# MLP products in a Strassen form on 2x2 blocks, tokens in two passes

## The chip, the cores and the metric

The kernel runs on one core of one Trainium2 chip, as one program. The metric is the device time of one execution in microseconds. The engines are TensorE (PE; its weight loads are shown as PEld), VectorE (DVE), ScalarE (ACT), GpSimd (POOL) and SyncE (SP), which issues nearly all DMAs from one queue, in order.

## The reference, cut to what matters

One layer of a decoder trunk for 2048 tokens of width 1024, all in float32. The change touches the W_out product, the MLP and the gated embeddings; what stands ahead of them (8 heads of softmax attention with a forget gate, "FoX", and 4 heads of a chunkwise "mLSTM") stays the same in what it computes.

```python
def reference(x, p, w_in, ..., w_up, w_down, w_ple, g_ple, w_ple_gate, g_final):
    ...
    mix = jnp.concatenate([fox_out, ml_out], axis=-1).astype(x.dtype)
    x = x + mix @ w_out[i]                                        # 2048x1024 @ 1024x1024

    hm = rmsnorm(x, g_mlp[i])
    x = x + jnp.square(jax.nn.relu(hm @ w_up[i])) @ w_down[i]     # 1024 -> 4096 -> 1024

    gate = jax.nn.sigmoid(rmsnorm(x, g_ple[i]) @ w_ple_gate[i])   # 1024x1024
    x = x + gate * (p[i] @ w_ple[i])
    return rmsnorm(x, g_final)
```

## The kernel before, in words

A float32 product is made of three float16 matmuls: each factor is split into a high half (the value rounded to float16) and a low half (the rest), and `PASSES` takes high x high, high x low, low x high. So one product of a 128-deep slice costs three matmuls, and every factor has to be split first: ACT writes the high half, DVE or POOL subtracts it for the low one.

The stages follow one another: norm of x and its transposes; four mLSTM heads (`ml_z` projects a head, `gates` makes the gate sums, then a loop over 16 chunks of 128 tokens); attention in pairs of heads, with a share of W_out between; the rest of W_out (`o`, L642 by `wo_token`); the MLP; the gates (`pg`, L991); the final norm.

The MLP goes over 16 blocks `jb` of 256 hidden columns. For each, `mlp_w` loads 1 MB of w_up (`prep_w`) and 1 MB of w_down (`prep_rows`) and makes a power-of-two scale, high and low halves, all of it while the block before is at work. `mlp_up` makes the hidden block of a group of 512 tokens (48 matmuls of 128x512, L1011), squares its relu and splits it; `mlp_down` multiplies it by the rows of w_down (48 matmuls, L1029) and adds each 128x512 result to x in SBUF (L1034). All 2048 tokens of x stay in SBUF (`x1`). The gates stage loads and splits w_ple_gate in four column blocks of 256 and runs 16 tokens tiles on each.

A scheduler sets the order of the instructions on each engine when the program is built, from the order in the source and from what it expects each to take; the buffers of a pool (`bufs=`) decide which load may start when. At run time every engine goes through its own list in order and waits at semaphores. The staging tile `st` has one buffer that all weight loads share.

## Time and profile before

| | us |
|---|---|
| median of 3 runs (lowest to highest) | 2996.92 (2991.71 to 3000.48) |
| profiled execution, span from first to last instruction | 2998.0 |
| norm, transposes | 0 to 33.6 |
| mLSTM, first part of it the projections of head 0 | 33.6 to 530 |
| attention and the first half of W_out | 530 to 1347 |
| second half of W_out, MLP | 1347 to 2784 |
| gates and final norm | 2784 to 2998 |

The profile lists each instruction with its engine, its line of the kernel and its tile. A chain of waits goes back from the last instruction to what released each one; a timeline merges like instructions into a row with its start, its duration and a count (x48). Busy times of PE overlap within a row, since matmuls are pipelined: what 48 of them cost is read from the start of one row to the start of the next.

### The profile page before, as it was taken

Reading aid. Unit: us, or ns where it says so; the run is one execution under the profiler, and the core shown is the slowest. Engines: PE = TensorE matmul, PEld = TensorE weight load, DVE = VectorE, ACT = ScalarE, POOL = GpSimd, SP = SyncE. Lnnn points to the kernel's source line nnn. Section 1 sums busy time; section 2 is a strip of 40 time slices with the busy share of each in tenths; the row PEclk is TensorE's granted clock in tenths of the full one; section 3 lists DMA queues with packets and bytes.
Section 4 is the critical chain, followed back from the end, with each engine's and each line's share of the span. In section 5 each row is a group of like instructions: output and inputs, shape, how many; then the busy total and the mean of one; then the engine's idle time right before and its main releaser. Section 6 shows DMA issues by size and latency. Waiting matters only on the chain. (4 is left out here: it accounts for less than half of the span.)

```text
span 2998.0 us, 43441 instructions
## 1 busy us (share of the span) xinstructions
PE 2747.0 (92%) x17141; PEld 1483.3 (49%) x17141; DVE 1676.0 (56%) x3764; ACT 1049.3 (35%) x1878; POOL 751.9 (25%) x529
## 2 busy tenths in 40 slices
PE   4998999889888787888899999999999999999996
PEld 2766767454453443443344444444444444444785
DVE  6464654666858667557754454444544544445526
ACT  6244444465655564553411111111111111114432
POOL 1001100233433343243122111111121111111454
PEclk9999999999999998999999999999999999999998
DMA  9112220486876797896700000000000000003513
GB/s 246 38 44 57 57 50 22 112 156 131 146 148 132 150 200 187 190 201 218 149 29 29 29 29 29 15 26 17 29 29 28 29 29 29 28 15 70 112 43 141
DMA packets 539869, 256.27 MB, mean 85 GB/s; under 512 B 433296, under 2 KB 511376, under 8 KB 539664
## 3 DMA queue, kind: packets, MB, share of 16 engines
q1 hardware_dynamic: 529904, 236.67, 34.8%
q10 hardware_dynamic: 9760, 16.82, 1.7%
q8 instruction: 134, 2.20, 0.3%
q14 instruction: 71, 0.58, 0.1%
HBM read 113.88 MB, written 32.60 MB: 49 GB/s over the span
## 5 line engine op out<-in xcount | busy, mean ns | idle before, releaser
L1029 PE MATMUL d<-wd_hl,hid 128*128 128x512 f16 x3072 | 677.2, 380 | 10.7 <-DVE x L1034 10.6
L1011 PE MATMUL h<-y1t,wu_hl 128*128 128x512 f16 x3072 | 673.5, 379 | 2.5 <-ACT y1y L201 2.5
L1029 PEld LDWEIGHTS <-hid 128*128 128x128 f16 x3072 | 301.1, 98 | 376.6 <-issue 16.8
L1011 PEld LDWEIGHTS <-wu_hl 128*128 128x128 f16 x3072 | 300.5, 98 | 365.2 <-ACT y1y L201 3.0
L1034 DVE SCALAR_TENSOR_TENSOR x<-d,fac,x 128x512 f32<-128x512 f32 x512 | 373.5, 747 | 132.2 <-PE d L1029 132.1
L1019 POOL TENSOR_TENSOR hid<-r,hid 128x512 f16<-128x512 f32 x128 | 174.7, 1365 | 772.3 <-ACT hid L1018 666.4
L1017 DVE SCALAR_TENSOR_TENSOR r<-h,r 128x512 f32<-128x512 f32 x128 | 88.3, 690 | 461.6 <-ACT r L1015 461.5
L1015 ACT ACTIVATE r<-h 128x512 f32<-128x512 f32 x128 | 76.0, 594 | 768.9 <-PE h L1011 768.9
L812 POOL TENSOR_TENSOR ph<-sp,ph 128x1024 f16<-128x1024 f32 x119 | 255.8, 2162 | 311.5 <-ACT ph L810 216.3
L272 PEld LDWEIGHTS <-yt 128*128 128x128 f16 x3072 | 245.0, 100 | 37.0 <-issue 15.0
L261 PE MATMUL zqk<-yt,wqk_hl 128*128 128x512 f16 x768 | 188.0, 392 | 27.0 <-DMA yt<-yy 27.0
L805 ACT ACTIVATE sp<-sp,nb,fs 128x1024 f32<-128x1024 f32 (+3 forms) x192 | 179.1, 982 | 50.4 <-DVE nb L802 34.9
L991 PE MATMUL pg<-wpg_hl,y2t 128*128 128x256 f16 x1536 | 173.3, 276 | 17.6 <-ACT emb L1110 13.6
L272 PE MATMUL zvo<-wvo_hl,yt 128*128 128x256 f16 x1536 | 174.7, 275 | 4.8 <-ACT wvo_hl L156 3.5
L782 PE MATMUL s<-K,Q 128*128 128x512 f16 (+3 forms) x320 | 117.5, 367 | 62.7 <-DVE mx L790 61.1
L991 PEld LDWEIGHTS <-y2t 128*128 128x128 f16 x1536 | 151.9, 99 | 39.1 <-issue 19.7
L810 ACT CAST ph<-sp 128x1024 f16<-128x1024 f32 x136 | 139.0, 1038 | 71.5 <-DMA pt<-ph 71.3
L827 PE MATMUL av<-vt,pt 128*128 128x129 f16 x1088 | 115.5, 229 | 49.2 <-DVE og L837 29.3
L790 DVE CUSTOM_DVE_ANT_0 sp<-s,bias,mx 128x512 f32<-128x512 f32 (+2 forms) x192 | 124.0, 646 | 17.8 <-POOL ph L812 5.1
L827 PEld LDWEIGHTS <-pt 128*128 128x128 f16 x1088 | 102.8, 102 | 53.1 <-issue 31.9
L261 PEld LDWEIGHTS <-wqk_hl 128*128 128x128 f16 x768 | 77.4, 101 | 104.0 <-ACT wqk_hl L156 24.9
L642 PEld LDWEIGHTS <-mix 128*128 128x128 f16 x768 | 74.1, 101 | 99.9 <-issue 26.8
(378 smaller groups left out, 3581.3 us busy)
## 6 DMA issues: line engine op xcount, KB each, us to landing
x<-in_x_dram SPq DMA_DIRECT2D x32, 512.0 KB, 4.6
wu_st<-in_w_up_dram SPq DMA_DIRECT2D x16, 1024.0 KB
wd_st<-in_w_down_dram SPq DMA_DIRECT2D x16, 1024.0 KB, 4.9
bias<-crow SPq DMA_DIRECT2D x16, 512.0 KB, 5.1
pled<-fox_st ACTq DMA_DIRECT2D x32, 256.0 KB, 3.0
wod<-spare ACTq DMA_DIRECT2D x32, 256.0 KB, 3.5
wos<-wod SPq DMA_DIRECT2D x32, 256.0 KB, 3.5
emb<-pled SPq DMA_DIRECT2D x64, 128.0 KB, 2.1
```

Of the source, the lines that this page charges most:

```text
L261: PE.matmul(ps, lhsT=hl[:, a, kt, m * P:(m + 1) * P], rhs=yT[g][b][:, kt, :], start=i == 0, stop=i == 3 * KT - 1)
L272: PE.matmul(ps[:, 0:n], lhsT=yT[g][b][:, kt, o:o + P], rhs=hl[:, a, kt, 0:n], start=i == 0, stop=i == 3 * KT - 1)
L790: V.tensor_tensor_reduce(out=st[u][:, o * P:(o + n) * P], in0=ps[:, 0:n * P], in1=bias[kb // 8][:, kb % 8 * P:(kb % 8 + n) * P], scale=1.0 ...
L805: A.activation(sl_, sl_, AF.Exp, bias=nb, scale=fs[:, 0:1])
L810: A.copy(ph[:, 0:1024], st[u])
L812: eng.tensor_sub(ph[:, 1024:2048], st[u], ph[:, 0:1024])
L827: PE.matmul(ar, lhsT=pt[:, o, :], rhs=vs, start=kb == 0, stop=False)
L991: PE.matmul(ps, lhsT=aT[t // 4][ya][:, kt, o:o + P], rhs=hl[:, wa, kt, :], start=i == 0, stop=i == 3 * KT - 1)
L1011: PE.matmul(ps, lhsT=wu[:, a, kt, m * P:(m + 1) * P], rhs=y1T[g][b][:, kt, :], start=i == 0, stop=i == 3 * KT - 1)
L1019: T.tensor_sub(hid[:, 1, m], r2, hid[:, 0, m])
L1029: PE.matmul(ps, lhsT=hid[:, a, m, t * P:(t + 1) * P], rhs=wd[:, b, m, hf * 512:(hf + 1) * 512], start=i == 0, stop=i == 5)
L1034: V.scalar_tensor_tensor(xs, ps, fac, xs, ALU.mult, ALU.add)
```

## The change

Both MLP products are made from 2x2 blocks. Of a product of blocks, eight block products become seven, on sums and differences of the blocks (`ORD_U`, `ORD_D`: the order in which the seven are made). The token side of a block pair is a pair of groups of 512 tokens, so the MLP runs in two passes over two groups each (`PAIRS`), and x of one pass at a time stays in SBUF; the other lies in DRAM (`xd`).

The sums of the weights are made once, in the first pass, for 16 blocks of w_up (`up_prep`) and 16 of w_down (`down_prep`): load 1 MB into the one buffer `raw`, scale it in place, make four sums, split seven blocks into halves of one buffer `poa` (`po()` gives its two halves in turn), and write them to DRAM (`wud`, `wdd`). Both passes read them back, 256 KB per step of w_up (`u_load`, three buffers) and 512 KB per two steps of w_down (`d_load`, two buffers). Since all sums need one common scale, `w_max` first reads all of both matrices for their largest value, in the chunk loops of the mLSTM, two 1 MB loads per four chunks.

W_out is done pass by pass, both column halves of a token tile together. The seven token blocks of the first pass are transposed into SBUF (`y_prep_sb`), those of the second are made from x in DRAM by way of `raw` and `poa`, written to DRAM (`y_prep_dr`) and loaded when the second pass starts. A step of the MLP is 12 matmuls of 128x512; steps of up and down alternate, those of down 17 steps behind. There are 32 x 7 steps of up and 2 x 8 x 7 x 2 of down. The gates run per token tile with all 1024 columns, on weights that are loaded and split during the last steps of down (`pg_prep`).

```diff
+    def w_max(i):
+        n, dn = divmod(i, 2)
+        st = wst.tile([P, 2 * D], F32, tag="st", name=f"mxs{i}", bufs=1)
...
+            V.tensor_reduce(mxd[:, n:n + 1], st, axis=AX.X, op=ALU.max,
+                            apply_absolute_value=True)
...
                 A.activation(jk, num[:, c, 0:MD], AF.Square, accum_out=ss[:, c:c + 1])
+                if c % 2 == 1:
+                    w_max(8 * h + c // 2)
...
+    raw = sl.tile([P, 2 * D], F32, tag="u", name="raw", bufs=2)
+    poa = sl.tile([P, 4 * D], F16, tag="u", name="poa", bufs=2)
...
+    def split(dst, src, every=0):
+        A.copy(dst[0], src)
+        cnt_lo[0] += 1
+        eng = V if every and cnt_lo[0] % every == 0 else T
+        eng.tensor_sub(dst[1], src, dst[0])
...
+    def up_prep(n):
...
+        SP.dma_start(out=raw.rearrange("p (k f) -> p k f", k=KT),
+                     in_=w_up[:, n * 256:(n + 1) * 256].rearrange("(k p) n -> p k n", p=P))
+        yield
+        for k in range(KT):
+            A.activation(raw[:, k * 256:(k + 1) * 256], raw[:, k * 256:(k + 1) * 256], AF.Copy,
+                         scale=msc[:, k:k + 1])
...
+        V.tensor_add(s4(sd, 0), a(1, 0), a(1, 1))
+        V.tensor_sub(s4(sb, 0), s4(sd, 0), a(0, 0))
+        yield
+        V.tensor_sub(s4(sb, 1), a(0, 0), a(1, 0))
+        V.tensor_sub(s4(sd, 1), a(0, 1), s4(sb, 0))
+        out_(pt, 0, 2)
+        yield
+        pt2 = po()
+        split(pair_hl(pt2), sb, 2)
+        yield
+        out_(pt2, 2, 2)
+        pt = po()
+        split(pair_hl(pt), sd, 2)
+        yield
+        out_(pt, 4, 2)
+        pt2 = po()
+        v = pt2[:, 0:D].rearrange("p (a k f) -> p a k f", a=2, k=4)
+        A.copy(v[:, 0], a(1, 1))
+        T.tensor_sub(v[:, 1], a(1, 1), v[:, 0])
+        yield
+        out_(pt2, 6, 1)
...
+    def y_prep_dr(t, rs):
...
+        def dst(k, t_, pt):
+            n = len(k)
+            st = po().rearrange("p (i s) -> p i s", s=P)[:, 0:8 * n]
+            SP.dma_start_transpose(out=st, in_=pt[:, 0:n * D])
+            SP.dma_start(out=ycd[k][:, :, t_ * P:(t_ + 1) * P], in_=st)
...
+    def u_step(k):
...
+        for kt in range(4):
+            for a, b in PASSES:
+                PE.matmul(ps, lhsT=wt[:, a, kt, :], rhs=yt[:, b, kt, :],
+                          start=fresh and m == 0, stop=m == 11,
+                          skip_group_check=True)
+                m += 1
+        u_load(k + 3)
...
+    for k in range(NU + OFF):
+        if k < NU:
+            n, pos = divmod(k, 7)
+            u_step(k)
+            if n == NF - 1:
...
+                SP.dma_start(out=Y[pk][:, 8 * j:8 * j + 8], in_=ycd[pk][:, 8 * j:8 * j + 8])
...
+        if k >= OFF:
+            d_step(k - OFF)
+        if k < NF * 7 - 7:
+            credit += BG_RATE
+            while credit >= 1:
+                credit -= 1
+                next(bg, None)
...
-    for b in range(4):
-        cs = slice(b * 256, (b + 1) * 256)
-        hl, pw = prep_w(w_ple_gate, [(b * 256, 256)], g_ple_t, f"wpg{b}")
```

On SP after the transposes of the first norm, before (`wqk`, `wvo`: weights of the next mLSTM head; `crow`, `mrow`, `wt`: gate rows on their way to DRAM and back):

```order
L128 DMA wqk_st<-in_w_in_dram 128x8x128 x2
L128 DMA wvo_st<-in_w_in_dram 128x8x128 x2
L380 DMA crow<-scr_1070 128x128
L128 DMA wqk_st<-in_w_in_dram 128x8x128 x2
L411 DMA mrow<-scr_1070 64x128
L491 DMA wt_1551<-mrow 128x16x128
```

and now, at the same place (`mxs`: the loads of `w_max`):

```order
L439 DMA mxs_1588<-in_w_up_dram 128x8x256
L433 DMA mxs_1631<-in_w_down_dram 128x2x1024
L439 DMA mxs_1674<-in_w_up_dram 128x8x256
L433 DMA mxs_1717<-in_w_down_dram 128x2x1024
L439 DMA mxs_1760<-in_w_up_dram 128x8x256
L433 DMA mxs_1803<-in_w_down_dram 128x2x1024
L439 DMA mxs_1846<-in_w_up_dram 128x8x256
L433 DMA mxs_1889<-in_w_down_dram 128x2x1024
L128 DMA wqk_st<-in_w_in_dram 128x8x128 x2
L380 DMA crow<-scr_1073 128x128
L128 DMA wvo_st<-in_w_in_dram 128x8x128 x2
L411 DMA mrow<-scr_1073 64x128
```

Eight loads of 1 MB that share the one staging buffer now stand ahead of the weights of head 1. On PE at this place 151 matmuls of the projections of head 1 (`zqk`) stood between the end of `gz` and the first chunk product of head 0 (`n`, L505 before), and now there are 95.

On SP in the middle of the first pass, one block of w_down on its way (`wring_16410` is the ring of `u_load`, `wring_16411` that of `d_load`, `wud_` and `wdd_` the sums in DRAM); before, one load of w_up and one of w_down stood here per block:

```order
L1133 DMA raw<-in_w_down_dram 128x2x1024
L1339 DMA wring_16411<-wdd_15674 128x2048
L1328 DMA wring_16410<-wud_15662 128x1024 x2
L1143 DMA wdd_15675<-poa 128x2x1024
L1339 DMA wring_16411<-wdd_15674 128x2048
L1143 DMA wdd_15675<-poa 128x2x1024
L1328 DMA wring_16410<-wud_15663 128x1024
L1143 DMA wdd_15675<-poa 128x2x1024
L1143 DMA wdd_15675<-poa 128x1024
L1133 DMA raw<-in_w_down_dram 128x2x1024
```

Loads into `raw`, writes of sums and loads for PE are now interleaved in one queue. From the first step of up on, 29 loads into `raw` for blocks of weights stand there, one to some 3.5 loads of `u_load`.

On SP where the second pass starts (`y_`: token blocks in SBUF, `ycd_`: the same in DRAM, `wud_15657`: block 0 of w_up again); before, nothing of the kind was there:

```order
L1239 DMA_TRANSPOSE poa<-poa 128x16x128
L1573 DMA y_16008<-ycd_15682 128x4096
L1240 DMA ycd_15683<-poa 2048x1x128
L1573 DMA y_16008<-ycd_15682 128x4096
L1239 DMA_TRANSPOSE poa<-poa 128x8x128
L1573 DMA y_16009<-ycd_15683 128x4096
L1240 DMA ycd_15684<-poa 1024x1x128
L1573 DMA y_16009<-ycd_15683 128x4096
L1573 DMA y_16010<-ycd_15684 128x4096
L1328 DMA wring_16410<-wud_15657 128x1024 x3
```

The last token blocks are transposed, written and loaded back ahead of the loads for the second pass. On PE all steps of down of the first pass stand ahead of the first step of up of the second.

## Rows read from the trace of the kernel before

**Rows 1.** The page: span, and what DMA moved in 40 equal slices.
```profile
span 2998.0 us, 43441 instructions
GB/s 246 38 44 57 57 50 22 112 156 131 146 148 132 150 200 187 190 201 218 149 29 29 29 29 29 15 26 17 29 29 28 29 29 29 28 15 70 112 43 141
```

**Rows 2.** Busy time by stage: stretch, length, PE, PEld, DVE, ACT, POOL, PEclk, DMA, GB/s.
```profile
1500.00:2784.00 1284.00, 1282.31 (x5936) 580.62 (x5935) 617.60 (x951) 230.70 (x341) 234.94 (x169) 1.00 0.10 29
2784.00:2998.00 214.00, 173.47 (x1538) 151.85 (x1536) 96.79 (x218) 70.70 (x209) 108.58 (x131) 0.93 0.36 101
```

**Rows 3.** The chain of waits in the MLP: start, duration, what.
```profile
2606.24 10.36 PE h L1011 x48
```

**Rows 4.** The chain of waits, where it leaves PE for one block.
```profile
2199.60 5.49 DMA wu_st<-in_w_up_dram
```

**Rows 5.** Groups by line and shape: count, busy time, mean ns, idle time before.
```profile
L812 POOL TENSOR_TENSOR ph<-sp,ph 128x1024 f16<-128x1024 f32 x119 | 255.8, 2162 | 311.5 <-ACT ph L810 216.3 <-DVE mx L790 26.1 <-DVE nb L802 25.3
...
L1019 POOL TENSOR_TENSOR hid<-r,hid 128x512 f16<-128x512 f32 x128 | 174.7, 1365 | 772.3 <-ACT hid L1018 666.4 <-issue 105.9
...
L810 ACT CAST ph<-sp 128x1024 f16<-128x1024 f32 x136 | 139.0, 1038 | 71.5 <-DMA pt<-ph 71.3
...
L1017 DVE SCALAR_TENSOR_TENSOR r<-h,r 128x512 f32<-128x512 f32 x128 | 88.3, 690 | 461.6 <-ACT r L1015 461.5
...
L1018 ACT CAST hid<-r 128x512 f16<-128x512 f32 x128 | 79.1, 618 | 118.3 <-DVE r L1017 118.3
...
L165 DVE TENSOR_REDUCE wd_mx<-wd_st 128x1 f32<-128x2048 f32 x16 | 36.5, 2283 | 1.4 <-DMA wd_st<-in_w_down_dram 1.2
...
L168 ACT ACTIVATE wd_hl<-wd_st,wd_sc 128x2048 f16<-128x2048 f32 x16 | 32.0, 2002 | 169.1 <-DVE wd_sc L121 157.8 <-DVE fac L1046 11.1 <-DMA y1t<-y1y 0.2
...
L1110 ACT ACTIVATE emb<-pg,invg 128x256 f32<-128x256 f32 x64 | 29.0, 457 | 4.3 <-PE pg L991 4.3
```

**Rows 6.** DMA issues: tiles, queue, count, size, median us from issue to landing.
```profile
wd_st<-in_w_down_dram SPq DMA_DIRECT2D x16, 1024.0 KB, 4.9
...
mixd<-mT SPq DMA_DIRECT2D x8, 512.0 KB, 3.4
...
y1t<-y1y SPq DMA_TRANSPOSE x16, 4.8
```

**Rows 7.** Timeline of PE around the gate sums: start, duration, what, [idle before].
```profile
136.72 12.49 PE L261 MATMUL zqk<-yt,wqk_hl 128*128 128x512 f16 x46
149.05 0.49 PE L357 MATMUL cps<-scr 128*128 128x192 f32 x2
...
163.09 12.47 PE L261 MATMUL zqk<-yt,wqk_hl 128*128 128x512 f16 x57
179.84 0.80 PE L505 MATMUL n<-va,wt 128*128 128x129 f32 x2 [4.28 <-DVE wt L502]
```

**Rows 8.** Timeline of SP's queue, same place.
```profile
80.00 1.00 SPq L128 DMA_DIRECT2D wqk_st<-in_w_in_dram  x2
```

**Rows 9.** Timeline of PE in W_out and at the MLP's start.
```profile
1347.01 41.83 PE L642 MATMUL o<-wo_hl,mix 128*128 128x512 f16 x192
...
1408.12 22.52 PE L642 MATMUL o<-wo_hl,mix 128*128 128x512 f16 x96 [5.55 <-DVE x L1069]
1433.13 10.52 PE L1011 MATMUL h<-y1t,wu_hl 128*128 128x512 f16 x48 [2.49 <-ACT y1y L201]
```

**Rows 10.** Timeline of SP's queue in the transposes of y.
```profile
1421.06 31.64 SPq L204 DMA_TRANSPOSE y1t<-y1y  x12
```

**Rows 11.** Timeline of PE: end of the MLP, and the last gate matmuls.
```profile
2784.14 5.40 PE L991 MATMUL pg<-wpg_hl,y2t 128*128 128x256 f16 x48
...
2972.32 2.78 PE L991 MATMUL pg<-wpg_hl,y2t 128*128 128x256 f16 x24 [1.47 <-ACT emb L1110]
```

**Rows 12.** Timeline of POOL, same columns, in W_out.
```profile
1372.08 3.59 POOL L150 TENSOR_TENSOR wu_st<-wu_st,wu_gs 128x2048 f32<-128x2048 f32 x1 [8.62 <-issue]
```

**Rows 13.** Timeline of DVE at the same moment.
```profile
1372.48 3.74 DVE L1075 TENSOR_TENSOR x<-x,wos 128x512 f32<-128x512 f32 x1 [3.80 <-DMA wos<-wod]
```

More of the change, by code (lines that the diff above doesn't have):

```diff
@@ new lines, in chain, with take @@
+    def chain(*gens):
+        for g_ in gens:
+            yield from g_
+    def take(gen, n):
+        for _ in range(n):
+            if next(gen, 0) == 0:
+                return False
+        return True
+    gen = chain(up_prep(0), up_prep(1))
+    for h in range(2):
+        for t in range(4):
+            wo_tok(0, h, t)
+            take(gen, 2)
+    y_tiles()
+    r0_ = rstds(ssx[0], "y1")
+    rs0 = [r0_[:, 0:4], r0_[:, 4:8]]
+    gen2 = chain(*(y_prep_sb(t, rs0) for t in range(4)))
@@ new lines, in hybrid_layer @@
+    take(gen, 99)
+    for h in range(2):
+        for t in range(4):
+            wo_tok(1, h, t)
+            take(gen2, 4)
+    take(gen2, 99)
+    r1_ = small.tile([P, 8], F32, tag="rs1", name="rs1", bufs=1)
+    V.tensor_copy(r1_, rstds(ssx[1], "y1b"))
+    rs1 = [r1_[:, 0:4], r1_[:, 4:8]]
+    hA = [tp.tile([P, 16, GT], F16, tag="T", name=f"hid{i}") for i in range(2)]
+    hB = wst.tile([P, 4 * D], F16, tag="st", name="hid2", bufs=1)
+    wA = whl.tile([P, 4 * D], F16, tag="hl", name="wring0", bufs=2)
@@ new lines, in hybrid_layer, with x_pair, gate_tok @@
+    xg = [whl.tile([P, 2, D], F32, tag="hl", name=f"xg{i}", bufs=2) for i in range(2)]
+    xg.append(wst.tile([P, 2, D], F32, tag="st", name="xg2", bufs=1))
+    nxg = [0]
+    def x_pair(h, q):
+        v = xg[nxg[0] % 3]
+        nxg[0] += 1
+        rows = slice((4 * h + 2 * q) * P, (4 * h + 2 * q + 2) * P)
+        SP.dma_start(out=v, in_=xd[0][rows, :].rearrange("(j p) c -> p j c", p=P))
+        return v
+    def gate_tok(pi, h, t, xt):
+        g = PAIRS[pi][h]
+        tok = 4 * g + t
+        yt = y2T[pi, h]
+        emb = qt(f"emb{tok}").rearrange("p i c -> p (i c)")
+        gate = qt(f"gate{tok}").rearrange("p i c -> p (i c)")
+        SP.dma_start(out=emb, in_=pled[tok * P:(tok + 1) * P, :])
+        ps = mmp.tile([P, 2, GT], F32, tag="d", name=f"pg{tok}", bufs=2)
+        for c in range(2):
+            m = 0
@@ new lines, in gate_tok @@
+                    m += 1
+            for i in range(2):
+                cs = slice(c * GT + i * 256, c * GT + (i + 1) * 256)
+                A.activation(gate[:, cs], ps[:, c, i * 256:(i + 1) * 256], AF.Sigmoid,
+                             scale=pwg_[2 * c + i])
+            cs = slice(c * GT, (c + 1) * GT)
+            T.tensor_mul(gate[:, cs], gate[:, cs], emb[:, cs])
+        V.tensor_add(xt, xt, gate)
+        A.activation(emb, xt, AF.Square, accum_out=ss3[:, tok:tok + 1])
+        T.tensor_mul(xt, xt, gfin)
@@ new lines, in hybrid_layer @@
+    pend = None
+    seq = [(pi, h, q) for pi in range(2) for h in range(2) for q in range(2)]
+    side = None
+    xq = {s: x_pair(s[1], s[2]) for s in seq[:3]}
+    for n, (pi, h, q) in enumerate(seq):
+        if pi:
+            xt = X[h][q]
+        else:
+            xt = xq.pop((pi, h, q))
+        if n == 0:
+            side = y2_sb(0)
+        if n == 2:
+            y2b[1] = yp.tile([P, 16, GT], F16, tag="y45", name="y2_1")
+            side = chain(side, y2_sb(1))
+        for j in range(2):
+            gate_tok(pi, h, 2 * q + j, xt[:, j])
+            next(side, None)
+            if n < 2:
+                pass
+        gate_end(pi, h, 2 * q + 1, xt)
+        if n + 3 < 4:
+            xq[seq[n + 3]] = x_pair(*seq[n + 3][1:])
+        if n == 3:
+            take(side, 99)
```

600 lines of the change are left out of this document (474 added, 126 removed).

## The prediction, made before the changed kernel ran

> **What bounds the kernel now.** I read the busy times by stage first, then the chain of waits, then PE's timeline at both edges of the MLP. From 1500 to 2784 us PE is busy 1282.3 of 1284 us at full granted clock; DVE, ACT and POOL have half or less [rows 2]. The chain agrees: it runs on PE alone, 10.36 us for 48 matmuls, 0.2158 us each [rows 3]. So this stage goes down in proportion to matmuls, as long as everything else stays under PE. At the edges it is otherwise: between the first W_out matmul at 1347.0 and the first gate matmul at 2784.1 lie 1437.1 us, and 6528 matmuls (384 of W_out, 6144 of the MLP) take 1408.8, so some 28 us are waits, the longest 5.55 and one of 2.49 for the first y [rows 9]. The gates stage takes 214 us, of which PE is busy 173 [rows 2]; 23 us follow the last gate matmul, which ends at 2975.1 [rows 11].
>
> **The change, part by part**, against the profiled span of 2998.0 us, 1.1 above the median of the runs shown.
>
> *Matmuls of the MLP.* 224 steps of up and 224 of down with 12 matmuls are 5376 for 6144: -768 x 0.2158 = **-165.7 us**. That is the whole gain, if PE never waits.
>
> *The maxima of the weights.* 32 loads of 1 MB, each with a DVE reduction, through one staging buffer: load 4.9 [rows 6] plus reduction 2.28 [rows 5], some 7.7 us each with the hand-over. Eight stand on SP ahead of the weights of head 1, whose load was issued at 80.0 [rows 8]; it now goes out at about 80 + 8 x 7.7 = 142, and its split weights are there some 18 us later (load 4.9, reduction 2.3, scaling by POOL 3.6 [rows 12], cast and subtraction 2 each, and small ones). At 136.7 PE used to go straight into the projections of head 1, 151 matmuls up to the first chunk product at 179.8 [rows 7]. Now it waits from 136.7 to about 149 for the gate sums, and to about 160 for the weights; of the 151 only 95 stand there, so 56 x 0.2158 = 12 us are done later, and the product itself comes a few us late: 14 to 18. Later, three chunk loops have 14 chunks in all without projections as filler, at six fillers or 1.3 us each: 17. Sum **+32**; from +10 (the chunk loops absorb it) to +60 (each of the four loops waits for its last loads).
>
> *W_out and the start.* The same 384 matmuls, 82.9 us. The seven blocks of the first pass are made under the second half of them, 41 us: 12 full transposes and 4 half ones, at 31.64/12 = 2.64 us [rows 10] 37 us; but each full one waits for one of two halves of `poa`, held for a cast 1.04, a subtraction 2.16 and a transpose 4.8, so 4 us apiece at best, 58 in all [rows 5, 6]. PE then waits 15 to 25 us. Before, this place had the 28 us of waits. I set the two equal: **0**, from -15 to +15.
>
> *First pass: the preparation of the weights.* It is a chain through one buffer `raw`, and on SP its loads stand in between those that PE needs, so PE can't run away from it: with three buffers of 256 KB it is at most three steps ahead. For w_up: load 5.49 [rows 4]; eight scalings of 128x256 at 0.457; three dependent sums at 0.69; cast 1.04; low half 2.16; then the write of that half of `poa`, 512 KB, 3.4; then the last block, cast 0.62 and low half 1.37, the last readers of `raw` [rows 5, 6]. Sum 19.7. For w_down the scaling is one instruction of 2.0 and the load 4.9: 17.6. Mean **18.7 us**. PE itself needs 24 x 0.2158 = 5.18 us for a step of up and one of down, and 3.5 such steps per load into `raw`: 18.1. So chain and PE are nearly level in the first pass.
>
> 29 blocks remain after the first step of up; then four tokens' blocks of the second pass, each three full rounds and a short one of transpose 4.8 and write 3.4 through the two halves of `poa` (28.6) and load, scaling and first split (7): 36; then a reload of 1 MB, 4.9. All that stands ahead of the second pass: 29 x 18.7 + 4 x 36 + 5 = 691 us. PE's own work there is 224 x 12 x 0.2158 = 580. So **+111 us**, mostly a gap at the end of the first pass, where only the tokens' blocks are left. Bounds: 18.1 per block, as PE paces it, and 29 per token give 646 (+66); 22.5 per block gives 802 (+222).
>
> *Second pass.* No preparation; DMA goes at 1.84 MB for up and as much for down per 36 us, 101 GB/s, where the start of this kernel moved 246 [rows 1]. DVE has per 36 us some 13 operations of 128x512 at 0.69 and 7 of twice that width, 19 us in all [rows 5]. **0**.
>
> *Gates.* 768 matmuls of 128x512, 165.7 us, where 1536 of 128x256 stand in 191 us from 2784.1 to 2975.1 [rows 11]; the weights are made under the last steps of down. Tail: sigmoid, product, sum and final scale of a whole row, which I estimate at 16 for 23. With 4 for the start: 186 for 214, **-28**; between -35 and -10.
>
> Sum: -165.7 + 32 + 0 + 111 - 28 = -51: span 2947, a run of **2946 us**.
>
> A rule that speaks against this. On the trace: a POOL multiplication of 3.59 us began at 1372.08, and a DVE addition of two SBUF tiles that began at 1372.48 ended with it after 3.74 us [rows 12, 13], though such an operation takes 0.69 [rows 5]. The Trainium skill, "SBUF — State Buffer" (Who interferes with whom), states it as a rule: DVE's second SBUF input and POOL go through one port pair, an exclusive lock. The trace agrees; what it would give is the second rival.
>
> **The rivals.**
>
> *Preparation hidden* (faster still). If low halves fall to DVE where POOL is busy, and casts never wait on ACT, the chain is PE's 18.1 and a token's blocks 29: +66. With +10 for the maxima and -10 for the start: -165.7 + 66 + 10 - 10 - 28 = -128, **2870 us**. For it: all durations used are means that hold waits. Against it: the order itself puts all steps of down of the first pass ahead of the second, which says that the tokens' blocks are late in any case.
>
> *The first pass turns into a queue of small waits* (slower). Per pair of blocks, 36 us of PE, POOL has some six subtractions of 128x1024 and five of 128x512, 20 us [rows 5]; DVE has 15 operations of 128x512 and two or three wider ones on two SBUF tiles, 14 us. If one blocks the other, as in rows 12 and 13, each of the five such operations on a block's chain can wait for a foreign one of up to 2.16; at 0.75 us each a block takes 22.5. DMA adds to it: a pair of blocks moves 9.4 MB in 37 us, 254 GB/s, the rate of the busiest slice so far [rows 1], so loads take longer than alone. 29 x 22.5 + 149 = 802, +222: -165.7 + 32 + 222 - 28 = +60, **3057 us**. It decides from 20.5 us per block on, where the sum is zero. For it: SP, ACT and DVE go in order, and an instruction of the chain stands behind ones that wait for PE. Against it: where the chain is late, PE's work is waiting for it and not the other way round.
>
> *Only the maxima and the start go wrong* (about even). With +60 for the maxima and +15 for the start beside the forecast's other terms: -165.7 + 60 + 15 + 111 - 28 = -8, a run of **2989 us**. For it: the loads of the maxima stand in SP's queue ahead of those that each head needs; against it: each head's loop has some 90 us for eight of them.
>
> **How the numbers follow.** Forecast 0.38, with its own range 2905 to 2985; preparation hidden 0.14; small waits 0.37; even 0.11, half of it within 0.3% (9 us), which is about what a measurement of this kernel can tell from no change. Faster 0.38 + 0.14 + 0.01 = 0.53, same 0.06, slower 0.41. The range reaches from the first rival to a little past the second: 2870 to 3080.
>
> **What would show it.** In the changed profile: PE without waits at 0.2158 us per matmul in the second pass, 580 us long; 29 loads into `raw` 18 to 19 us apart in the first; one gap of PE of some 70 to 80 us ahead of the second pass, ended by a DMA of `y`; the gates stage near 186 us; the weights of head 1 near 160 us. I am wrong if the loads into `raw` are over 20.5 us apart, if PE waits throughout the first pass rather than at its end, or if the mLSTM loops lose more than 60 us.

## The result, and the profile after

The changed kernel takes 3237.99 us (median of 4 runs, 3233.26 to 3245.07); the kernel before took 2994.59 us beside it (4 runs, 2991.71 to 3000.48). The ratio is 1.081 [1.0791, 1.0829]: 8% slower, where 2946 us was forecast, and outside the range of 2870 to 3080. The profiled execution is 245.3 us longer than that of before [rows 1].

The page of the changed kernel; `PEclk` is TensorE's granted clock in tenths, slice by slice:

```profile
span 3243.3 us, 41139 instructions
PEclk9888988999989899989899998999959999999999
GB/s 235 118 93 105 130 75 118 74 108 145 136 167 125 132 184 210 192 192 242 230 202 178 217 185 202 198 211 199 213 229 259 191 104 101 99 103 162 135 138 85
```

In the MLP most slices moved 29 GB/s before; now those of the first pass (20 to 30, of 81 us each) move 178 to 230, and those of the second go from 259 down to 99. The busy times by stage (columns as in [rows 2]; the stages are the gate sums of the mLSTM, its chunk loops, W_out, first pass, second pass):

```profile
127.00:180.00 53.00, 22.11 (x414) 15.03 (x411) 34.88 (x67) 16.16 (x16) 4.55 (x3) 0.58 0.28 80
180.00:594.00 414.00, 358.51 (x2320) 250.63 (x2319) 237.32 (x502) 159.48 (x415) 36.93 (x19) 0.90 0.37 101
1440.00:1580.00 140.00, 100.56 (x388) 40.83 (x386) 83.23 (x124) 57.94 (x85) 35.43 (x22) 0.87 0.87 234
1580.00:2419.00 839.00, 630.04 (x2688) 270.20 (x2689) 530.78 (x519) 291.59 (x389) 341.69 (x178) 0.90 0.63 202
2419.00:3047.00 628.00, 595.32 (x2689) 265.49 (x2689) 323.72 (x375) 98.27 (x117) 144.85 (x73) 0.97 0.48 145
```

Where PE was busy 1282.3 of 1284 us before, it is now busy 630 of 839 in the first pass, and no other engine is near its limit there: DVE has 63%, POOL 41%, ACT 35%, the DMA engines 63%. Nothing is full, and PE waits: that is the picture of a chain that depends on itself, which the experiments below test. Set against the terms of the sum, with the times at which PE starts its first matmul of each stage:

| term | forecast | measured |
|---|---|---|
| matmuls of the MLP, 768 fewer | -165.7 | -165.7 |
| maxima: start of W_out's second half 1347.0 -> 1440.6 | +32 | +93.6 |
| W_out and the start: 139.5 - 82.9 of matmuls - 28.3 of waits before | 0 | +28.3 |
| first pass: 839.2 for 580.1 | +111 | +259.1 |
| second pass: 627.6 for 580.1 | 0 | +47.5 |
| gates: 196.5 for 213.9 | -28 | -17.4 |
| sum | -51 | +245.4 |

Two terms carry most of the miss, 148 and 62 of 296 us. What PE waits for, over the whole span (us in total, times, longest):

```profile
PE u16X L1360 <- DMA y<-ycd: 69.1, 1, 69.1
...
PE d L1440 <- DVE x_va L1448: 44.8, 17, 5.8
PE d L1440 <- DVE x_og L1448: 40.7, 19, 6.6
PE d L1440 <- DMA wring<-wdd: 38.1, 11, 8.7
PE n L541 <- DVE wt L538: 34.8, 16, 15.0
PE o L682 <- DVE xr L1268: 30.9, 12, 6.3
```

The gap ahead of the second pass is there as forecast, 69.1 us for 70 to 80, ended by a DMA of `y`. But 124 us more stand in small waits of `d`, 111 of them in the first pass, which should have run level with its preparations.

**The preparations' chain.** Of the 32 loads into `raw`, the 16 of w_down (duration of the issue min/median/max, first and last start):

```profile
L1133 SPq DMA_DIRECT2D raw<-in_w_down_dram x16: 373/426/462, 1592.8 to 2251.8; - x16
```

28 intervals of two kinds of blocks lie between them: (2251.8 - 1592.8) / 28 = 23.5 us per block, where 18.7 was forecast and 20.5 was the limit. Before the first of them lie 13 us, behind the last 167.5 for the last block, the four tokens and the reload (18.7 + 149 forecast, which is right as a sum). So 28 x 4.8 = 135 us and these 13 are the 148. One block of w_up, as the chain of waits has it (start, duration, what):

```profile
1926.88 7.21 DMA raw<-in_w_up_dram
...
1934.59 2.89 ACT raw L1081 x7
...
1937.57 0.69 DVE sd L1106
1938.26 1.56 DVE sb L1109
1939.82 1.02 DVE sb L1107
1940.83 1.74 issue
...
1942.59 2.58 POOL poa L1065
1945.19 3.05 DMA wud<-poa
...
1951.07 8.64 DMA raw<-in_w_up_dram
```

The steps and their order are those of the sum, and from load to load they take 24.2 us for the 19.7 forecast. The 1.74 us that the chain gives without a releaser are the end of the third sum, which ran to 1941.38 (below), and ACT's cast, which the forecast has at its 1.04:

```profile
1941.41 1.04 ACT L1062 CAST poa<-sb 128x1024 f16<-128x1024 f32 x1 [2.91 <-DVE sb L1107]
```

So in this block the load takes 1.7 us more than forecast (7.2 for 5.49 [rows 4]; 8.6 the next time), the three sums 1.7 more (3.8 for 2.1), and POOL's low half 0.4 more (2.6 for 2.16 [rows 5]). The hand-overs between the steps, which the forecast did not price, take 1.4, of which 0.9 lie on SP ahead of the next load. Scaling, write and the last block are 0.9 shorter. What the sums meet, DVE first, then POOL, at the same moment:

```profile
1938.17 1.64 DVE L1109 TENSOR_TENSOR sb<-raw 128x512 f32<-128x512 f32 x1
1939.74 1.64 DVE L1107 TENSOR_TENSOR sb<-sd,raw 128x512 f32<-128x512 f32 x1
```
```profile
1938.06 2.77 POOL L1103 TENSOR_TENSOR poa<-raw,poa 128x512 f16<-128x512 f32 x2 [9.51 <-ACT poa L1100]
```

Each sum takes 1.64 us beside a subtraction on POOL, of the same block; the sum that began at 1937.57, ahead of it, took 0.69. It is [rows 12, 13] over again, but the block stands in its own way: POOL makes the first low half while DVE makes the sums.

**The maxima.** SP's queue behind the transposes of the norm (compare [rows 8]), then PE at the gate sums (compare [rows 7]):

```profile
80.29 0.37 SPq L439 DMA_DIRECT2D mxs<-in_w_up_dram  x1
88.16 0.37 SPq L433 DMA_DIRECT2D mxs<-in_w_down_dram  x1
...
125.25 0.37 SPq L439 DMA_DIRECT2D mxs<-in_w_up_dram  x1
140.98 0.37 SPq L433 DMA_DIRECT2D mxs<-in_w_down_dram  x1
148.08 0.99 SPq L128 DMA_DIRECT2D wqk_st<-in_w_in_dram  x2
```
```profile
157.06 0.98 PE L357 MATMUL cps<-scr 128*128 128x192 f32 x2 [17.72 <-DVE scr L354]
...
170.25 6.52 PE L261 MATMUL zqk<-yt,wqk_hl 128*128 128x512 f16 x18 [8.65 <-ACT wqk_hl L156]
```

7.9 and 7.2 us from load to load, as forecast; one interval of 15.7 (125.25 to 140.98) comes on top, and the weights of head 1 are there at 170 for 160. The first chunk product comes at 197.9 for 179.8: the forecast had 14 to 18 for this, and it is 18. The miss lies behind it: the four chunk loops take 396.0 us (start of the first product to start of the last) for 336.4, +59.6 where 17 was forecast, and another 16 come up to the start of W_out. SP at the first head's end, then PE, then PE at the same place before:

```profile
275.60 0.37 SPq L433 DMA_DIRECT2D mxs<-in_w_down_dram  x1
...
278.25 0.43 SPq L527 DMA_DIRECT2D wt<-mrow  x1
```
```profile
296.45 0.80 PE L541 MATMUL n<-va,wt 128*128 128x129 f32 x2 [14.98 <-DVE wt L538]
```
```profile
265.83 0.80 PE L505 MATMUL n<-va,wt 128*128 128x129 f32 x2 [11.62 <-DVE wt L502]
```

The rows `wt` that the next head's first product needs are loaded behind the last maximum of this head, and PE waits 15.0 us for them. The sum had the loads ahead of the *weights* of a head, not ahead of its gate rows. But PE waited 11.6 us for `wt` here before, so only 3.4 of these are new. From the first product of one head to that of the next it takes 12.6, 10.2 and 29.1 us more than before, and the last loop 7.6 more: no single wait carries the 60.

### The profile page after: what moved, and what is told of

Same layout as the page of the kernel before. It is cut to its first block, busy times and chain, and to the rows that moved or that the text cites. A ratio compares the mean times of both kernels' runs of the same rounds, so it can differ in the third digit from the quotient of the medians.

```text
span 3243.3 us, 41139 instructions
## 1 busy us (share of the span) xinstructions
PE 2680.9 (83%) x15605; PEld 1359.7 (42%) x15605; DVE 1935.7 (60%) x3609; ACT 1203.2 (37%) x1943; POOL 968.1 (30%) x522
## 4 chain that ended last, share of the span: by engine, by line
PE 23%; DMA 18%; DVE 11%; issue 6%; POOL 6%; ACT 5%; SPq 1%; DVEq 0%; POOLq 0%; ACTq 0%
PE d L1440 7%; DMA raw<-in_w_up_dram 3%; DMA poa<-poa 3%; DMA pt<-ph 3%; DMA raw<-in_w_down_dram 3%; PE pg L1646 2%; POOL poa L1065 2%; ACT raw L1081 1%; PE om L682 1%; DMA wud<-poa 1%; POOL hid L1065 1%; DMA ycd<-poa 1%; DVE tb L1151 1%; PE s L824 1%; DMA wdd<-poa 1%
## 5 line engine op out<-in xcount | busy, mean ns | idle before, releaser
L1440 PE MATMUL d<-wring,hid 128*128 128x512 f16 x2304 | 554.1, 394 | 112.8 <-DVE x_og L1448 40.7
L1360 PEld LDWEIGHTS <-wring 128*128 128x128 f16 x2688 | 265.8, 100 | 453.0 <-issue 109.2
L1440 PEld LDWEIGHTS <-hid 128*128 128x128 f16 x2304 | 231.0, 101 | 413.9 <-issue 128.4
L1646 PE MATMUL pg<-wpg,y 128*128 128x512 f16 x768 | 170.0, 381 | 11.0 <-ACT gate L1651 11.0
L1448 DVE SCALAR_TENSOR_TENSOR x_og<-d,msc,x_og 128x1024 f32<-128x1024 f32 x96 | 122.4, 1278 | 75.3 <-PE d L1440 75.1
L1448 DVE SCALAR_TENSOR_TENSOR x_va<-d,msc,x_va 128x1024 f32<-128x1024 f32 x96 | 122.6, 1278 | 66.5 <-PE d L1440 66.4
L867 PE MATMUL av<-vt,pt 128*128 128x129 f16 x1088 | 117.6, 230 | 39.0 <-DVE og L877 19.6
L1065 POOL TENSOR_TENSOR hid<-rA,hid 128x1024 f16<-128x1024 f32 x32 | 71.0, 2219 | 241.8 <-ACT hid L1062 120.9
L682 PE MATMUL o<-wo_hl,mix 128*128 128x512 f16 x384 | 99.9, 422 | 37.7 <-DVE xr L1268 30.9
L824 PE MATMUL s<-KL,Q 64*128 64x512 f16 (+3 forms) x320 | 121.1, 378 | 0.0
L1646 PEld LDWEIGHTS <-y 128*128 128x128 f16 x768 | 75.5, 98 | 105.4 <-issue 17.4
```

Source lines behind the costliest of these rows:

```text
L682: PE.matmul(ps, lhsT=mg[t // 4][ya][:, 4 * r + kt, o:o + P], rhs=hl[:, wa, kt, :], start=i == 0, stop=i == 11)
L824: PE.matmul(ps[:, 0:n * P], lhsT=Qt[r0:r0 + 64, qs], rhs=KL[r0:r0 + 64, ks], start=False, stop=not diag)
L867: PE.matmul(ar, lhsT=pt[:, o, :], rhs=vs, start=kb == 0, stop=False)
L1065: eng.tensor_sub(dst[1], src, dst[0])
L1360: PE.matmul(ps, lhsT=wt[:, a, kt, :], rhs=yt[:, b, kt, :], start=fresh and m == 0, stop=m == 11, skip_group_check=True)
L1440: PE.matmul(ps[:, j], lhsT=h[:, a, t * P:(t + 1) * P], rhs=w[:, f, c, :], start=fresh and m == 0, stop=m == 5, skip_group_check=True)
```

## The experiments

Times are of one run where no interval is given; the changed kernel's profiled execution took 3245.07. The kernel before took 2996 to 3011 us beside the experiments, so a difference of some 15 us between the times of two of them tells nothing; stages and blocks are read within a trace. "Start" is the time at which W_out's second half starts.

### The maxima

**Taken away, but for two loads.**

```diff
-                if c % 2 == 1:
-                    w_max(8 * h + c // 2)
+                if h == 0 and c in (1, 3):
+                    w_max(c // 2)
```

> Left out: 30 of the 32 loads and reductions that look for the largest weight (the scale comes from the first block of each matrix). Theory 'the maxima cost the mLSTM stage its 94 us': the first matmul of the second W_out half goes back from 1440 us to about 1350, the whole to about 3150; first and second pass stay at 839 and 628 us. Rival 'the mLSTM loops lose to the new order of the projections, whatever is loaded': under 40 us come back.

Measured: 3150.57 us (3011.41 for the kernel before beside it), start 1341.3 for 1440.6, first pass 844.0, 23.6 us per block. The chunk loops of this kernel, against the second line of the stages above:

```profile
180.00:520.00 340.00, 322.22 (x2264) 230.87 (x2265) 185.96 (x455) 155.50 (x412) 30.87 (x16) 0.97 0.19 43
```

The first theory holds: all 94 us up to the start are the maxima's, and nothing of the first pass is. With them go 58 GB/s of DMA, and the granted clock comes back from 0.90 to 0.97.

**Only the reductions made small; and the reductions whole, but in two buffers of half the size.**

```diff
-            V.tensor_reduce(mxd[:, n:n + 1], st, axis=AX.X, op=ALU.max,
+            V.tensor_reduce(mxd[:, n:n + 1], st[:, 0:64], axis=AX.X, op=ALU.max,
...
-            V.tensor_reduce(mxu[:, n], sv, axis=AX.X, op=ALU.max, apply_absolute_value=True)
+            V.tensor_reduce(mxu[:, n], sv[:, :, 0:8], axis=AX.X, op=ALU.max, apply_absolute_value=True)
```

> Left out: 31/32 of each reduction for the largest weight (a strip of the block is looked at); the 32 loads of 1 MB through the one staging buffer stay. Theory 'the head's weights wait behind the loads in queue and buffer' (a load is still 5 us, so eight in a row are 40 us for 62): of the 92 us that the maxima cost, 30 or less come back; second W_out half starts at 1410 us or later. Rival 'DVE time: 32 x 2.28 = 73 us in a stage where the chunk loops need DVE': 60 us or more come back, start at 1380 or earlier.

```diff
-        st = wst.tile([P, 2 * D], F32, tag="st", name=f"mxs{i}", bufs=1)
...
+        for j in range(2):
+            st = pool.tile([P, D], F32, tag="mT", name=f"mxs{i}_{j}", bufs=2)
...
+                V.tensor_reduce(mxd[:, 2 * n + j:2 * n + j + 1], st, axis=AX.X, op=ALU.max,
```

> The maxima are taken in halves of 512 KB through the two 4 KB buffers that hold the transposed mLSTM output, so the staging buffer of the heads' weights is free; same loads in bytes, same DVE elements, results as in the change. Theory 'queue and buffer': start of the second W_out half from 1440 to 1390 or earlier. Rival 'DVE time': within 15 us of 1440, since the reductions are all there.

Measured: 3199.70 and 3191.53; start 1387.3 and 1388.0. The two give back the same 53 us, though one keeps the single buffer and the other the reductions. The first falls between its two expectations, the second is as its theory has it. The chunk loops, first without reductions, then with two buffers:

```profile
180.00:563.00 383.00, 346.77 (x2336) 240.65 (x2335) 196.04 (x493) 159.97 (x416) 36.85 (x19) 0.96 0.38 108
```
```profile
180.00:563.00 383.00, 337.23 (x2303) 236.39 (x2302) 245.78 (x507) 157.02 (x414) 35.87 (x17) 0.95 0.39 107
```

DVE has 50 us more work in the second, and the length is the same to the us: what sets these 53 us is not DVE's time as such. What both edits shorten is the cycle of load and reduction through the one staging buffer; that it is this cycle is inferred from the two together. About 40 us are left either way. PE's waits for `wt` in the chunk loops, before, with two buffers, and with short reductions:

```profile
PE n L505 <- DVE wt L502: 16.1, 3, 11.6
```
```profile
PE n L542 <- DVE wt L539: 35.9, 5, 13.9
```
```profile
PE n L541 <- DVE wt L538: 10.5, 3, 7.4
```

With two buffers the gate rows account for some 20 of the 40; with short reductions they wait less than before and 40 us are lost all the same. So what the rest consists of stays open.

### The first pass

**No preparations but the first ones.** PE reads the same sums for all blocks.

```diff
     def bg0():
-        yield from up_prep(2)
-        for b in range(NBK):
-            yield from down_prep(2 * b)
-            yield from down_prep(2 * b + 1)
...
+        yield from down_prep(0)
+        yield from down_prep(1)
         for t in range(4):
```

> Left out: the preparation of the weight sums in the first pass but for one block of each matrix, which all steps then load again and again (the loads for PE stay in number and size, the results are not those of the layer). Theory 'the chain of preparations through one buffer sets the first pass': first step of up to second pass falls from 839 us to 580 to 620, the blocks of the second pass's tokens being made early; the whole to about 3000. Rival 'DVE's evacuations and the ring loads hold PE up by themselves': it stays over 700.

Measured: 2988.97 us (3011.41 for the kernel before beside it); first pass 559.4, second 654.6. (The border has moved, here and in the runs with the last reader moved ahead: the last steps of down of the first pass run within the second, so only the sum compares with the changed kernel's, 1214 for 1467 us.)

```profile
1575.00:2134.00 559.00, 543.10 (x2481) 244.13 (x2482) 301.77 (x342) 106.50 (x128) 157.04 (x80) 0.98 0.53 154
```

PE is busy 97% with the same reads of sums from DRAM, the same work on hidden blocks and the same tokens' blocks. So 253 us are the preparations'.

**The last reader of `raw` first.** In each block the seventh copy and subtraction, and its write, move ahead of the two splits of the sums.

```diff
         pt2 = po()
-        split(pair_hl(pt2), sb, 2)
-        yield
-        out_(pt2, 2, 2)
-        pt = po()
-        split(pair_hl(pt), sd, 2)
-        yield
-        out_(pt, 4, 2)
-        pt2 = po()
         v = pt2[:, 0:D].rearrange("p (a k f) -> p a k f", a=2, k=4)
...
         out_(pt2, 6, 1)
+        pt = po()
+        split(pair_hl(pt), sb, 2)
...
```

> The last block read from raw is split right after the sums are made, ahead of the splits of the sums, so that the next load starts some 9 us earlier; work and results as in the change. Theory 'latency: a block's 23.5 us is the serial chain from one load into raw to the next': 18 us or less per block, first pass 839 -> 680 to 720. Rival 'throughput: DVE, POOL and their lock, or DMA, are used up at this rate': 22 us or more per block, first pass over 800.

Measured: 3121.13 us; first pass 689.2, second 656.9, sum 1346 for 1467.

```profile
L1133 SPq DMA_DIRECT2D raw<-in_w_down_dram x16: 383/384/457, 1581.6 to 2071.8; - x16
```

17.5 us per block, as the theory of latency has it. Not an instruction, a byte or a buffer is less than in the changed kernel: order alone gives 117 us. What sets the first pass of the changed kernel is a chain through one buffer, not a shortage of an engine or of DMA.

**The low halves of the preparations made on ACT**, copies in place of the subtractions of POOL, and of DVE where it makes them.

```diff
+    def split_a(dst, src):
+        A.copy(dst[0], src)
+        A.copy(dst[1], src)
...
-            T.tensor_sub(w4[1][:, i], src[:, i], w4[0][:, i])
+            A.copy(w4[1][:, i], src[:, i])
...
-        split(pair_hl(pt2), sb, 2)
+        split_a(pair_hl(pt2), sb)
...
```

> On the changed kernel itself: the low halves of the weight sums as second copies by ACT (POOL's and DVE's subtractions in the preparation left out; results are not those of the layer). The 23.5 us of a block are 4.8 more than the forecast's sum. If a block's own operations block each other (DVE's dependent sums take 1.47 to 2.62 for 0.69 while POOL makes the low half of the same block), the sums fall back to 0.7 and a block to 20 us or less, the first pass by 80 us or more. If they are not it, only the difference of the instructions on the path goes, about 1.04 for 2.4 once and 0.62 for 1.2 once: 21.5 us or more.

Measured: 3129.12 us; 19.6 us per block, first pass 723.7, both within what was expected if a block's own operations block each other. The sums of one block, in the changed kernel (count, busy us, mean ns), and here, where all lines stand four lower:

```profile
L1151 DVE TENSOR_TENSOR tb<-raw,td 128x512 f32<-128x512 f32 x12 | 31.4, 2620 | 0.0
L1107 DVE TENSOR_TENSOR sb<-sd,raw 128x512 f32<-128x512 f32 x11 | 18.0, 1640 | 0.0
L1109 DVE TENSOR_TENSOR sb<-raw 128x512 f32<-128x512 f32 x11 | 16.2, 1470 | 0.0
```
```profile
L1155 DVE TENSOR_TENSOR tb<-raw,td 128x512 f32<-128x512 f32 x15 | 16.1, 1072 | 0.0
...
L1111 DVE TENSOR_TENSOR sb<-sd,raw 128x512 f32<-128x512 f32 x13 | 8.9, 684 | 0.0
...
L1113 DVE TENSOR_TENSOR sb<-raw 128x512 f32<-128x512 f32 x13 | 8.9, 684 | 0.0
```

With POOL out of the way the two sums of w_up take the 0.69 us of the forecast, that of w_down 1.07: 1.5 to 1.7 us less per block, (1640 + 1470 - 2 x 684) ns for w_up and 2620 - 1072 for w_down. Another 1.9 is the low halves themselves, if ACT's copies take their 1.04 and 0.62 in place of 2.16 and 1.37 [rows 5]; that is an estimate. The two make some 3.5 of the 4.0 us that a block is shorter. The Trainium skill, "SBUF — State Buffer" (Who interferes with whom), says that a DVE instruction with two SBUF inputs and a POOL instruction that reads SBUF share one read interface, and that the order of issue decides who waits. The trace agrees with the first: two of these sums take 0.68 us with POOL's reads of the block gone, and 1.47 and 1.64 with them. No run here varies the order of issue alone.

**The hidden blocks' low halves made on ACT**, in the same manner, the preparations' own left on POOL.

```diff
-            split(pair_hl(s), rA)
+            split_a(pair_hl(s), rA)
...
```

> Left out: the subtraction for the low halves of the hidden blocks, which POOL makes; ACT writes a second copy in its place (so POOL has 8 us less of 20 per pair of blocks; results are not those of the layer). Rival 'POOL and DVE block each other': a block's preparation falls from 23.5 to 21 us or less, the first pass by 60 us or more. Theory 'latency of the chain itself': a block stays within 1 us of 23.5 and the first pass within 30 us of 839.

Measured: 3204.71 us; 22.4 us per block, first pass 806.6: just past the bounds of the second expectation (1 and 30 us), far from the first. Foreign subtractions on POOL cost a block 1.1 us, the block's own 4.0, queueing and duration together: a block is mostly in its own way.

**No loads for the steps of down** after the first two; matmuls of down read what lies in the ring.

```diff
-        SP.dma_start(out=w, in_=wdd[b % NBK][POS_D.index(ORD_D[pos])]
-                     .rearrange("p f c -> p (f c)"))
+        if k < 2:
+            SP.dma_start(out=w, in_=wdd[b % NBK][POS_D.index(ORD_D[pos])]
+                         .rearrange("p f c -> p (f c)"))
```

> Left out: all loads of w_down sums for PE after the first two, 110 of 512 KB (PE multiplies by the two blocks in the ring; results are not those of the layer). In the first pass DMA then moves about 7.6 MB per pair of blocks instead of 9.4. If DMA shared with the ring loads makes the chain's loads and writes longer (7.2 us for a block of w_up that alone takes 5.5), a block falls from 23.5 to 22 us or less and the first pass by 40 us or more; if the chain is not slowed by DMA, a block stays within 0.7 us of 23.5 and only PE's own 38 us of waits for these loads go, which the chain then hides: first pass within 15 us of 839.

Measured: 3203.02 us; 22.7 us per block, first pass 810.3. It falls between the expectations. 56 loads of 512 KB less in the first pass, 29 MB, shorten a block by 0.8 us. But the loads into `raw` themselves are no shorter in the mean: from issue to landing those of w_up take 6.8 us (median) for 7.2 in the changed kernel, those of w_down 6.0 for 5.4. So these reads are not what makes the loads longer than the 5.49 and 4.9 of the forecast, and where the 0.8 us come from is not shown.

**The early reader and the hidden blocks on ACT together.**

> The early last read of raw, and the low halves of the hidden blocks as second copies by ACT (the subtraction by POOL left out; results are not those of the layer). Theory 'with the long chain gone, POOL and DVE's shared time is what is left' (POOL 20 and DVE 14 us of every 35 us pair): a block falls from 17.5 us to 15.5 or less. Rival 'still the chain's own latency': within 0.7 us of 17.5.

Measured: 3081.60 us; 16.7 us per block, passes 654.5 and 653.8. Also between the expectations. A block is now made faster than PE uses one, 18.1 us, and yet the pass is longer than PE's matmuls in it, 2497 or 539 us: 28 x 16.7 and the 167 for the last block, the tokens and the reload are 635 already, if those still take what they took.

### W_out

**The loads of x and of the sums `wod` issued on ACT's queue**, not behind SP's transposes.

```diff
-            SP.dma_start(out=xt, in_=x[tok * P:(tok + 1) * P, :])
+            A.dma_start(out=xt, in_=x[tok * P:(tok + 1) * P, :])
...
-        SP.dma_start(out=e, in_=wod[tok * P:(tok + 1) * P, :].rearrange("s (i c) -> s i c", i=2))
+        A.dma_start(out=e, in_=wod[tok * P:(tok + 1) * P, :].rearrange("s (i c) -> s i c", i=2))
```

> The loads of x and of the kept half of W_out for each token tile are issued by ACT instead of SP, where the transposes of the first pass's blocks stand ahead of them. If these loads hold W_out up, the stretch from its second half to the first step of up goes from 139 us to 115 or less; if it is DVE's order (evacuations behind sums that wait for poa), it stays within 8 us of 139. The passes are unchanged, 839 and 628 us.

**One token's blocks of the first pass for four** under W_out, zeros for the others.

```diff
+    for m_ in (1, 2, 3, 4, 5, 6, 7):
+        V.memset(Y[m_][:, :, :, P:], 0.0)
+    gen2 = chain(*(y_prep_sb(t, rs0) for t in range(1)))
```

> Left out: three of the four tokens' blocks of the first pass that are made and transposed under the second half of W_out (zeros in their place; results are not those of the layer). If these blocks hold W_out up, by DVE's order and the two halves of poa, its second half to first step of up goes from 139 us to 110 or less; if W_out waits for its own buffers of x, it stays over 128. Passes unchanged.

Measured: 3255.13 and 3250.57 us; the stretch from W_out to the first step of up takes 144.0 and 131.6 for 139.5. Neither edit gives the stretch back. With the second, the waits for `xr` go from 30.9 to 22.3 us in 6, and others take their place. By what was expected these point at DVE's order and at the two buffers of x, but the second run settles less than it should: the seven memsets that write its zeros take DVE 1.34 us each in this stretch. What holds it is not found.

### What the form is worth, and how far it can be mended

**Neither maxima nor preparations**: the first two edits together.

> Left out: 30 of the 32 maxima and, in the first pass, all weight sums but those of one block of each matrix (the loads for PE stay; results are not those of the layer). It shows what the seven products for eight are worth when what they need costs nothing: if the two losses are all there is, 2987 - 88 = 2900 us, some 100 under the kernel before; if the second pass and W_out's start keep growing in their place, over 2930.

Measured: 2898.63 us, as expected if the two losses are all there is, and 104 less than the kernel before (3002.40, median of 7 runs beside it). The two passes:

```profile
1485.00:2043.00 558.00, 542.06 (x2481) 243.71 (x2482) 303.51 (x342) 106.78 (x128) 156.05 (x80) 0.99 0.54 154
2043.00:2700.00 657.00, 634.97 (x2899) 284.89 (x2898) 363.90 (x414) 108.30 (x135) 150.85 (x74) 0.99 0.46 143
```

1215 us for 1160 of matmuls: 55 us of waits and clock belong to the form as it is written, with no preparation beside it. Of the 307 us by which the two passes of the changed kernel are over 1160, 252 are thus the preparations'. The two losses add up to within the spread: 87 us without maxima, 249 without preparations, 339 without both, each from the median of 3238; set against the kernel before beside each, 104 and 266 for 347.

**The early reader and the maxima in two buffers**, nothing left out.

> The early last read of raw and the maxima through their own buffers together; nothing left out. If the two causes are independent, 117 and 47 us add up: 243 - 164 leaves some 75 to 85 us over the kernel before (ratio 1.025 to 1.03). If a shorter mLSTM stage or a denser first pass shifts a wait into the other (the same staging and DMA queue), under 140 us come back in all (ratio over 1.033).

Measured: 3065.36 us (4 runs, 3061.32 to 3075.33), ratio to before 1.0221 [1.0192, 1.0251]; start 1387.3, passes 683.6 and 652.6. It is 63 us over the kernel before, where 75 to 85 were expected of two independent causes: neither takes from the other.

**Then all low halves of the preparations on DVE**, none on POOL:

```diff
-            T.tensor_sub(w4[1][:, i], src[:, i], w4[0][:, i])
+            V.tensor_sub(w4[1][:, i], src[:, i], w4[0][:, i])
...
-        split(pair_hl(pt), sb, 2)
+        split(pair_hl(pt), sb, 1)
...
```

> Nothing left out: early last read, maxima through their own buffers, and all low halves of the weight sums on DVE instead of POOL (1.23 for 2.4 us each, and no POOL operation of the preparation left to block DVE; DVE gets 7 us more per pair of blocks). If the lock inside a block costs what the sums' lengths say, a block falls from 17.4 to 15 us or less and the first pass from 684 to 640 or less: about 3015. If DVE's queue is what a block waits for, it rises, and the first pass with it.

**then the squares of three of four hidden blocks on ACT**, as DVE is now the busiest but PE:

```diff
-            V.scalar_tensor_tensor(r, r, 0.0, r, ALU.max, ALU.mult)
+            A.activation(r, r, AF.Relu)
+            A.activation(r, r, AF.Square)
```

> e14 with the squares of three of four hidden blocks made by ACT (relu, then square, 0.6 us each) instead of one DVE operation on two SBUF inputs; nothing left out. If DVE is the engine that a block waits for in e14, the first pass falls by another 10 us or more; if it is the chain's loads and writes, within 8 us of e14.

Measured: 3047.25 and 3023.94 us, first pass 652.0 and 623.4, second 676.7 and 684.8. With DVE for POOL a block keeps its 17.4 us, where 15 or less was expected; the first pass is still 32 us shorter, but the second is 24 longer, so the two together gain 7. DVE was busy for 526 of the 652 us, and taking the squares from it makes a block 0.75 us shorter (16.7) and the first pass 29, for 8 in the second.

**then each head's maxima one head earlier**, the first eight behind the projections of head 0:

```diff
+        for i in range(8):
+            w_max(i, mb)
...
-                if c % 2 == 1:
-                    w_max(8 * h + c // 2, mb)
+                if c % 2 == 1 and h < MH - 1:
+                    w_max(8 * (h + 1) + c // 2, mb)
```

> e15 with the maxima one head earlier (eight in the projections of head 0, none in the last chunk loop); nothing left out. The mLSTM stage still ends some 36 us late. If each head's loop is late by its own share of loads and reductions, 10 us or more come back (start of the second W_out half at 1372 or earlier, the whole at 3014 or less); if the loads only collide earlier, with the gate sums of head 0, within 6 us of e15.

**and W_out's loads on POOL's queue:**

```diff
-            SP.dma_start(out=xt, in_=x[tok * P:(tok + 1) * P, :])
+            T.dma_start(out=xt, in_=x[tok * P:(tok + 1) * P, :])
...
```

> e16 with the loads of x and of the kept half of W_out issued by POOL, whose queue is nearly empty there; nothing left out. On ACT's queue they changed nothing (144 us for 139), ACT being in order behind its own work. If the issue of these loads is what W_out waits for, its second half to the first step of up falls from 135 to 115 us or less and the whole under 3000; if it is the two buffers of x and DVE's order, it stays within 6 us of 135, and the whole does not come under the kernel before.

Measured: 3031.12 us (4 runs), 1.0108 [1.0087, 1.013], and 3040.05 (4 runs), 1.0151 [1.013, 1.0171]. Moving the maxima moves the wait: the first chunk product now comes at 205.3 for 190.7, and the start gains 4 us, 1378.5 for 1382.5, where 10 were expected of loops that are late by their own loads. POOL's queue gives nothing either (141.0 us from W_out to the first step). No version that leaves nothing out beats the kernel before; the best two are some 1% slower (3023.94 for 3000.41 in one run each, and the 1.0108).

## Why the prediction was wrong

- *What bounds the kernel* and *matmuls*: right. PE was the bound, 768 matmuls less are there, and without maxima and preparations the form gains 104 us. That is less than 165.7: 55 us of its own waits and some 27 at W_out, both set to 0, stand against 17 from the gates.
- *First pass*: this step failed. The mechanism was right (a chain through `raw`, level with PE, and a last gap of 69 us; the early reader shows the chain), its size was not: the term of 18.7 us per block measured 23.5, and the pass came out at +259 for +111. The sum priced each operation by what it takes where it runs nearly alone. In the chain the sums met the block's own subtraction on POOL (+1.5 to 1.7, from their lengths with and without it), and foreign subtractions came between (1.1, shown by taking them away). The loads took 7.2 and 5.4 us for 5.5 and 4.9, 1.1 more in the mean; PE's reads for down are not the reason (6.8 and 6.0 without them), and the reason stays open. Side by side these are 3.8 of 4.8; whether they add up no run shows. Hand-over between the steps, at no price in the sum, is 1.4 us in the one block shown. And since chain and PE were level at 18.7 and 18.1, each excess counted in full, 28 times. The rows for it were on the table [rows 12, 13]: they stood as a rival at 0.37 and 22.5 us, where they should have stood in the sum. (In those rows the addition ended 0.55 us behind the multiplication, not with it.)
- *The second rival*, the queue of small waits, is what happened: 839 us for its 802. Its place is right, its cause in part: what it saw as foreign operations is mostly the block's own split. Its total of 3057 was still 181 short, for want of the maxima, W_out and the second pass.
- *Maxima*: failed too, by size and by place. +94 for +32 with a top of +60. The start of head 0 was right, 18 us for 14 to 18. The four loops lost 60 for 17, and another 16 came behind them. The cycle through one buffer, eight times some 7.7 us, was set against a loop of some 90 us and got no price of its own there; shortening this cycle gives 53 of the 94 us back. How the rest divides stays open.
- *W_out and the start*: set at 0, +28; outside its bounds of 15, and the cause stays open.
- *Second pass*: set at 0, +48. Some 12 us are the other loads of `y` (6.1 and 5.5 for `u16Z` and `u16Y`), 15 are matmuls at a mean granted clock of 0.97; the rest is in small waits.
- *Gates*: -17 for -28, inside the bounds.
- Of the three signs named for a wrong forecast two came: loads over 20.5 us apart, and waits of PE throughout the first pass. The third, over 60 us lost in the mLSTM loops, is at its limit: 59.6 in the loops, 78 with the late start of head 0.
- Two sums in it are slightly off and change nothing: the steps of w_up add up to 19.8 and not 19.7, and 14 chunks at 1.3 us to 18 and not 17.

## What to carry to other kernels

When the gain is taken from the engine that was the bound, ask first which chain through one buffer is now level with it; two paths that come out within a few per cent of each other are no cover: here every excess of the chain was paid in full and once per block. Price such a chain with the durations that its operations show beside each other, not alone: here an f32 sum of two SBUF tiles cost 0.69 us alone, and three of them 1.5 to 2.6 beside POOL. And look in such a chain for the last reader of the buffer first: moving one copy and one subtraction ahead was worth 117 us, more than the whole form gains.

## What was not expected of the hardware

After a wait, matmuls can run at half their speed, on work that ran at full speed just before. PE in W_out, then the granted clock in two of these stretches (eighth number):

```profile
1521.00 2.75 PE L682 MATMUL o<-wo_hl,mix 128*128 128x512 f16 x12 [2.57 <-DVE xr L1268]
1527.77 5.28 PE L682 MATMUL o<-wo_hl,mix 128*128 128x512 f16 x12 [4.02 <-DVE xr L1268]
1533.89 2.75 PE L682 MATMUL o<-wo_hl,mix 128*128 128x512 f16 x12 [0.84 <-DVE xr L1268]
```
```profile
1521.10:1523.70 2.60, 2.60 (x12) 1.07 (x11) 1.58 (x2) 0.81 (x1) 0.00 (x0) 1.00 1.23 225
1527.90:1533.00 5.10, 5.10 (x12) 1.66 (x11) 0.95 (x1) 2.19 (x2) 1.35 (x1) 0.50 0.99 214
```

12 matmuls take 2.75 us at a granted clock of 1.00 (2.4 GHz), and 5.28 at 0.50 (1.2 GHz) behind a wait of 4.02 us. Behind waits of 2.57 and 0.84 they keep the upper level here. In this stretch PE is busy 100.6 us with 388 matmuls worth 83.7: of the 56 us by which it is longer some 17 are clock, and 39 are waits. A wait of PE can so cost more than its length. The first pass has a mean clock of 0.90 too; what that costs there is not shown, since the chain of the preparations paces it.
